# A block's scan in two or three bursts instead of four, with the small work around it chained behind the bursts

## The chip, the cores and the metric

The kernel runs on one core of a Trainium2 chip. The time is the device time of one execution in microseconds (us); three runs of the kernel before gave 1520.81, 1521.10 and 1523.07 us, median 1521.1 us. The five engines are PE (TensorE, matmuls; PEld is its loading of weights), DVE (VectorE), ACT (ScalarE), POOL (GpSimd) and SP (SyncE, which here issues DMAs). Each works through its own instructions in order and waits at semaphores for the others.

## What is computed

One layer of a hybrid model on 128 context tokens and 1024 latent tokens, 1152 in all, of width 1024, in float32. Four GLA heads (keys of 64) and four HGRN heads (keys of 128) scan the tokens forwards and backwards, and a ConvFFN follows. Per head the scan is this recurrence, with its own gates in each direction; the context tokens also give the new states:

```python
def chunk_gated_linear(q, k, v, log_f, s0):
    '''S_t = diag(exp(log_f_t)) S_{t-1} + k_t v_t^T ; o_t = S_t^T q_t'''
    ...
    scores = jnp.einsum('bhnid,bhnijd,bhnjd->bhnij', q, decay, k)
    o_intra = jnp.einsum('bhnij,bhnjv->bhniv', scores, v)
    ...
def bidir_scan(q, k_fwd, k_bwd, v, logf_fwd, logf_bwd, s0_fwd, s0_bwd):
    ...
    return o_f + flip(o_b), s_f, s_b
...
    h = rmsnorm(x, norm1) * (1 + scale1) + shift1
    mix, new_gla, new_hgrn = hybrid_mixer(h, ...)
    x = x + gate1 * mix
    h = rmsnorm(x, norm2) * (1 + scale2) + shift2
    x = x + gate2 * conv_ffn(h, ...)
```

The shifts, scales and gates come from a product of a conditioning vector with `w_ada` (1024 x 6144), in three groups A, B and C of 2048 columns. A is needed at the start, B and C after the scan.

## The kernel before

**Stages.** Up to 87 us the kernel loads the tokens, computes group A of the conditioning, normalises, and makes the first projections. From 87 to about 645 us six groups of heads are scanned (`groups`, n = 0 to 5): groups 0 and 1 are GLA with two heads each (64 rows per head), groups 2 to 5 HGRN with one head each (128 rows). Then come the output projection and the ConvFFN, which the change leaves alone.

**A block.** A group takes its 1152 tokens in three blocks of 384 (`ORDER`, from the last to the first). `levels` scans a block by a tree of seven levels, 0 to 6: at level l, runs of 2^l tokens are joined in pairs. Each level has a part on three engines. `mixed` (L917, ACT) copies the halves of the keys or queries that meet at this level into one tile `m`. `update` (L927, L929, L933, DVE) multiplies the gates of a run onto Q, the keys k and the gates fb of the next level. And PE forms the scores of the level with many matmuls of 32 output rows (L964, output `lv`); `keep` (L978, L982, DVE) puts those that belong to the level into the tile of scores S by a mask. The matmuls of two levels form a *burst* (`burst`, L948): 48 instructions in HGRN, 96 in GLA, under high priority and held behind the projection named in `anchor["paced"]`. A block has four bursts: the diagonal (called level -1) with level 0, levels 1 and 2, 3 and 4, 5 and 6.

**The fills.** Between the bursts PE works on projections: `proj_d_steps` (L625, tiles of 128x384), `proj_t_steps` (L639, v, 128x256) and later the output projection (L777, 128x512). Each tile is the sum of three products of split operands (h1h x wh, h1l x wh, h1h x wl). `stream` hands them out so that at every half slot (eight slots per block, n and bi naming the group and the block) a goal of columns is reached (`GOALS`). Their weights are loaded by SP into two `raw` buffers (`load_w`, L129, L131), rounded by ACT into `wh` (L133), and the rest computed by POOL into `wl` (L69); a `raw` buffer is free when `wl` is done.

**The small work.** After each block its state products follow (`state_steps`): for each of three chunks of 128 tokens two transposes of keys (L1025), a copy to `kt` on ACT (L1028), and the products with v (L1032), one chunk after the other, since `ps_x` has one buffer. The results update the states `st` (L1044, L1049, DVE). When a group is scanned, its outputs are formed while the next group runs (`out_steps`: L1066 to L1069, L1092, L1106, a norm on ACT and POOL, transposes L1116, products with the output gate and a store). `gates` prepares the gates and keys of the next block; in GLA it begins with two matmuls (L868) from a tile `lr` loaded by DMA. The place of this work in the slots is a table in the code, and a scheduler orders each engine from it by priority.

**The conditioning pieces.** Groups B and C come in 32 pieces of 128x1024 from `w_ada`, each loaded by `ada_load` (L1191) and multiplied by `ada_product` (L1201, four matmuls of 32 rows, eight records in the trace). They begin in group 2, one behind a burst; five go through `raw`, 27 through free buffers of the pool `v`.

Of the kernel before, what the change touches and what calls it, by code (L numbers as in the profile page):

```python
# [28 lines left out]
BURST_AHEAD = 1000  # L29
NLOW = 5  # L30
# [19 lines left out]
def kernel(ctx: ExitStack, tc: tile.TileContext, ins, outs, stop=None):  # L50
# [161 lines left out]
    seq_w_out(4, 5)  # L212
# [92 lines left out]
    pjp = pool(es1, "pj", 13)  # L305
# [299 lines left out]
    ktp = pool(es1, "kt", 2)  # L605
    mp = pool(es1, "m15", 3)
    stp = pool(es1, "stt", 23)
# [214 lines left out]
    for n in range(2, 6):  # L822
        part_g(n - 2)
        m = groups[n]
        for into, nm in ((m.f, "fj"), (m.bb, "bj"), (m.q, "qj")):
            part_cols(into, nm)
        if n % 2 == 0:
            m.vpair = groups[n + 1].vpair = []
            part_v(m.vpair)
    part_g(4)  # L830
# [27 lines left out]
    def gates(u, b):  # L858
# [3 lines left out]
        if u.gla:  # L862
            lrs = op_.tile([P, BL], F32, name="lr", tag="on")
            nc.sync.dma_start(lrs, scr_lr[b])
            pss, bcs = [], []
            for d in range(2):
                ps = ps_o.tile([P, BL], F32, name="o", tag="o")
                mm(ps, u.wup[:, d, :], lrs, start=True, stop=True)  # L868
# [29 lines left out]
        return fb, k, k0  # L898

    def levels(u, b, fb, k, k0):  # L900
# [46 lines left out]

        def burst(*parts):  # L948

            widths = [LB << max(lev - NLOW, 0) for lev, _, _ in parts]  # L950
            pss = [ps_lv.tile([P, 3 * sum(widths)], F32, name="lv", tag="lv") for _ in u.heads]
# [5 lines left out]
            with tc.high_priority(offset=BURST_AHEAD):  # L957
                for (lev, keys, src), got in zip(parts[::-1], strips[::-1]):
                    for i in range(3):
                        for j in range(P // LB):  # L960
                            js = slice(j * LB, (j + 1) * LB)
                            for ps, (r0, r1) in zip(got, u.heads):
                                with tc.issue_after(last.ins) if last is not None else nullcontext():
                                    last = mm(  # L964
                                        ps[js, i, :],
                                        keys[r0:r1, i * P + j * LB : i * P + (j + 1) * LB],
# [20 lines left out]

        k_0 = mixed(kf_, 0)
        (diag, s0), last = burst((-1, k0, q), (0, k_0, Q))
        for SL_, ps in zip(SL, diag):  # L990
            nc.scalar.activation(SL_, ps, AF.Copy, scale=2.0 if u.gla else 1.0)
        keep(0, s0)
        update(0)
        yield last
        for lev in (1, 3, 5):
            ka, qa = mixed(kf_, lev), mixed(Qf_, lev)
            update(lev)
            kb = mixed(kf_, lev + 1)
            yield last
            strips, last = burst((lev, ka, qa), (lev + 1, kb, Q))  # L1000
            for n in range(2):
                keep(lev + n, strips[n])
            update(lev + 1)
            if lev == 3:
                for S_, SL_ in zip(S, SL):
                    for j in range(LB, P, LB):
                        nc.scalar.activation(S_[j : j + LB, :, j : j + LB], SL_[j : j + LB], AF.Copy)
            if lev == 5:
# [3 lines left out]
            yield last  # L1012
        yield last

    def state_steps(u, b, k):

        tl = u.tot[b]
        for i in (2, 1, 0):
# [28 lines left out]
            if b == 0 and i == 0:  # L1047
                for c in range(7):
                    nc.vector.scalar_tensor_tensor(  # L1049
                        u.stf[c + 1],  # L1050
                        u.stf[c],
                        u.tot[c // 3][:, 1, c % 3 : c % 3 + 1],
                        u.stf[c + 1],
                        op0=ALU.mult,
                        op1=ALU.add,
                    )
# [56 lines left out]
    def out_second(u, i, b, on):  # L1113
        pt = ps_o.tile([P, BL], F32, name="o", tag="o")
        for j in range(3):
            nc.tensor.transpose(pt[:, j * P : (j + 1) * P], on[:, j, :], ident)  # L1116
# [6 lines left out]
        if u is groups[2] or u is groups[4]:  # L1123
# [11 lines left out]
    def out_steps(u):  # L1135


        if u.gla:
            for b, (first, second) in enumerate(((7, 9), (10, 12), (15, 17)) if u.tau == 0 else ((9, 11), (12, 14), (15, 17))):
                yield "half", first  # L1140
# [1291 lines left out]
```

## Time and profile before

| | |
|---|---|
| median of three runs | 1521.1 us |
| span of the profiled execution | 1515.2 us |
| of it, the scan stage | 87 to 645 us |
| PE busy in the span | 1464.7 us (97%) |
| PE busy in the scan stage | 544.62 of 558.00 us |
| bursts (L964) | 72: 12 HGRN blocks and 6 GLA blocks with four each |

A row of the profile names line, engine, operation and tiles (out<-in), and its shapes. In a timeline the first two numbers are start and duration. Matmuls are pipelined, so their durations overlap: two consecutive projections start 0.17 us apart while each lasts 0.34. How long a stretch of PE took is therefore read from one start to another. A float32 matmul leaves two records, a projection or a transpose one: a burst of 24 instructions shows as x48.

### The profile page before, as it was taken

To read this page: it belongs to the slowest core of one execution; us is meant where nothing else is said; L and a number is where in the kernel's file an instruction comes from. 1 tells how busy PE (TensorE), PEld (TensorE's weight loads), DVE (VectorE), ACT (ScalarE), POOL (GpSimd) and SP (SyncE) were. 2 spreads that over 40 slices of the span, in tenths; PEclk is the share of its full clock that TensorE was granted. 3 is DMA by queue.
4 is the path that set the end of the run, shared out by engine and by line. 5 is a ranking of instruction groups with operands and counts; after the bars stand their busy time and mean duration, and the time that the engine had idled before them with its cause. 6 is when DMAs were issued, how large, how long until landed. Compare 5 with 4: busy or idle time off the path is not lost.

```text
span 1515.2 us, 31139 instructions
## 1 busy us (share of the span) xinstructions
PE 1464.7 (97%) x12509; PEld 1247.6 (82%) x12509; DVE 1145.1 (76%) x1735; ACT 781.1 (52%) x1519; POOL 705.0 (47%) x537
## 2 busy tenths in 40 slices
PE   6999999999999999899998999999999999999998
PEld 2898998999898988777776888888888877888886
DVE  3766566565565767755699999999999999689575
ACT  3575667555455455613765444444444444466444
POOL 1602122334333241222229999999999996100001
PEclk9999999999999999999999999999999999999999
DMA  9311111335535463967642745445644567989762
GB/s 341 134 44 48 45 57 52 117 98 171 162 97 184 120 203 121 334 247 251 219 142 89 244 115 144 119 119 139 196 119 139 169 154 215 371 267 368 241 191 115
DMA packets 173802, 253.79 MB, mean 167 GB/s; under 512 B 11828, under 2 KB 113698, under 8 KB 171738
## 3 DMA queue, kind: packets, MB, share of 16 engines
q1 hardware_dynamic: 150455, 173.52, 36.0%
q0 software_dynamic: 22592, 77.60, 16.6%
q8 instruction: 98, 1.61, 0.5%
q10 hardware_dynamic: 611, 0.68, 0.1%
q14 instruction: 46, 0.38, 0.1%
HBM read 191.93 MB, written 82.90 MB: 181 GB/s over the span
## 4 chain that ended last, share of the span: by engine, by line
PE 79%; DVE 7%; DMA 5%; ACT 3%; issue 3%; POOL 2%; SPq 0%; POOLq 0%; DVEq 0%; ACTq 0%
PE u L1777 24%; PE mm L625 15%; PE xb L2279 8%; PE yb L2279 6%; PE mm L639 5%; PE x L2009 4%; PE lv L964 3%; DVE acc L1943 3%; PE mm L777 2%; PE yb L2333 2%; PE u L1544 2%; PE x L1032 1%; PE mm L519 1%; DMA raw<-in_w_in_dram 1%; PE ada L1201 1%
## 5 line engine op out<-in xcount | busy, mean ns | idle before, releaser
L1943 DVE SCALAR_TENSOR_TENSOR acc<-u,convc,acc 128x945 f32<-128x945 f32 (+2 forms) x352 | 426.9, 1218 | 8.9 <-ACT acc L1931 1.8
L69 POOL TENSOR_TENSOR wl<-raw,wh 128x1024 fp32r<-128x1024 f32 x42 | 103.0, 2466 | 249.8 <-ACT wh L133 194.2
L625 PE MATMUL mm<-h1h,wh 128*128 128x384 f32 x528 | 185.0, 350 | 1.3 <-ACT qj L528 1.3
L625 PE MATMUL mm<-h1l,wh 128*128 128x384 f32 x528 | 179.0, 339 | 0.0
L625 PE MATMUL mm<-h1h,wl 128*128 128x384 f32 x528 | 179.0, 339 | 0.0
L927 DVE TENSOR_TENSOR Q<-Q,fb 128x384 f32<-128x384 f32 x126 | 81.9, 650 | 82.4 <-PE lv L964 81.4
L69 POOL TENSOR_TENSOR wul<-sr,wuh 128x512 fp32r<-128x512 f32 (+1 forms) x64 | 115.0, 1799 | 38.6 <-ACT wuh L1759 38.6
L69 POOL TENSOR_TENSOR wul<-ra,wuh 128x1024 fp32r<-128x1024 f32 x43 | 110.0, 2559 | 6.6 <-ACT wuh L133 6.5
L917 ACT ACTIVATE m<-k 128x384 f32<-128x384 f32 x126 | 70.2, 557 | 79.9 <-DVE k L929 37.2
L2243 POOL TENSOR_TENSOR sq<-sq,mhalf 128x1 f32<-128x1 f32 x9 | 11.1, 1231 | 205.8 <-DVE sq L2242 205.8
L625 PEld LDWEIGHTS mm<-h1h,wh 128*128 128x128 f32 x528 | 99.5, 188 | 6.2 <-issue 3.9
L625 PEld LDWEIGHTS mm<-h1l,wh 128*128 128x128 f32 x528 | 99.5, 188 | 0.6 <-issue 0.2
L625 PEld LDWEIGHTS mm<-h1h,wl 128*128 128x128 f32 x528 | 99.3, 188 | 0.8 <-issue 0.5
L639 PE MATMUL mm<-wh,h1h 128*128 128x256 f32 x288 | 83.8, 291 | 1.5 <-ACT v L664 1.5
L929 DVE TENSOR_TENSOR k<-k,fb 128x384 f32<-128x384 f32 x126 | 74.2, 589 | 12.3 <-ACT m L917 7.2
L639 PE MATMUL mm<-wh,h1l 128*128 128x256 f32 x288 | 80.4, 279 | 0.0
L639 PE MATMUL mm<-wl,h1h 128*128 128x256 f32 x288 | 80.4, 279 | 0.0
L133 ACT ACTIVATE wh<-raw 128x1024 fp32r<-128x1024 f32 x50 | 52.8, 1058 | 38.5 <-PE mm L625 11.6
L1971 ACT ACTIVATE u2p<-u 128x512 f32<-128x512 f32 x44 | 26.5, 602 | 77.3 <-PE u L1777 76.7
L1759 ACT ACTIVATE wuh<-ra 128x1024 fp32r<-128x1024 f32 x42 | 44.3, 1054 | 36.6 <-issue 22.1
L2045 POOL TENSOR_TENSOR acc<-acc,acc 128x1152 f32<-128x1152 f32 x22 | 60.0, 2730 | 5.0 <-DVE acc L1943 5.0
L1759 ACT ACTIVATE wuh<-sr 128x512 fp32r<-128x512 f32 (+1 forms) x63 | 48.7, 773 | 23.1 <-PE x L2009 16.4
(385 smaller groups left out, 4464.1 us busy)
## 6 DMA issues: line engine op xcount, KB each, us to landing
ra<-in_w_ffn_up_dram SPq DMA_DIRECT2D x84, 256.0 KB, 3.5
raw<-in_w_in_dram SPq DMA_DIRECT2D x32, 512.0 KB, 4.5
v<-in_w_ada_dram SPq DMA_DIRECT2D x27, 512.0 KB, 5.1
scr_g<-acc POOLq DMA_DIRECT2D x22, 576.0 KB, 5.6
scr_s<-late POOLq DMA_DIRECT2D x11, 1024.0 KB, 4.3
scr_t<-in_w_ffn_down_dram POOLq DMA_DIRECT2D x16, 704.0 KB, 7.3
wa<-in_w_ada_dram SPq DMA_DIRECT2D x16, 512.0 KB, 5.3
scr_t<-in_w_ffn_down_dram POOLq DMA_DIRECT2D x2, 2816.0 KB, 12.5
```

The costliest lines, as they stand in the source:

```text
L69: return eng.tensor_tensor(out, full, hi.bitcast(F32), op=ALU.subtract)
L625: anchor["fill"] = mm(ps, a[:, kt, :], h[kt][b], start=(n == 0), stop=(n == 23))
L639: anchor["fill"] = mm(ps, h[kt][t // 3][:, ts_], a[:, kt % 4, :], start=(n == 0), stop=(n == 23))
L917: nc.scalar.activation(aps(t, 0, [[2 * h, NB], [h, 2], [1, h]]), aps(src, 0, [[2 * h, NB], [BL + h, 2], [1, h]]), AF.Copy)
L927: nc.vector.tensor_tensor(qm, qm, aps(ff_, 2 * h - 1, [[BL - h, 2], [2 * h, NB], [0, h]]), op=ALU.mult)
L929: nc.vector.tensor_tensor(km, km, aps(ff_, BL + 2 * h - 1, [[-(BL + h), 2], [2 * h, NB], [0, h]]), op=ALU.mult)
L1759: return lambda: nc.scalar.activation(hi, raw, AF.Copy), lambda eng: split_lo(eng, lo, raw, hi)
L1777: last = mm(dst, w_slot(c, a, x)[:, kt, :], HB[y][b][:, kt, :], start=(start and n == 0), stop=(stop and n == 11), skip_group_check=True,)
L1943: last = nc.vector.scalar_tensor_tensor(o, u3[:, r0 + dy : r1 + dy, c0 + dx : c1 + dx], wc(3 * (dy + 1) + dx + 1), o, op0=ALU.mult, op1=AL ...
L2009: last = mm(pk, HB[h]["p"][:, 4 * half + kt, :], aps(flat(W[x]), a * 512 + kt * P, [[(b - a) * 512, 2], [1, P]]), start=(half + kt + n == ...
L2045: last = nc.gpsimd.tensor_tensor(accg, accg, accu, op=ALU.mult)
L2279: anchor["down"] = mm(banks[i][:, cs], w[a][:, ts_], w[b][:, 512 + cs.start : 512 + cs.stop], start=(start and j == 0 and n == 0), stop=(j ...
```

## The change

A block's levels go in fewer bursts: a table `BURSTS` names the levels after which a burst is issued. In GLA it has levels -1 to 2, then 3 and 4, then 5 and 6; in HGRN -1 to 2, then 3 to 6. The matmuls are the same. Level 6 reads the keys themselves in place of a mixed copy. More mixed copies wait for one burst, so the pool `m15` grows from 3 to 6 buffers and `kt` from 2 to 3; `pj` (projection results) shrinks from 13 to 11 and `stt` from 23 to 18.

`state_beats` takes the place of `state_steps` up to the second block of group 4: all of a block's key transposes stand directly behind one burst and all its products behind the next, using columns of the burst's own bank beside `ps_x`. `out_beats` places the outputs of groups 0 to 3 behind bursts by a table `OUT_SLOTS`. GLA's gate matmuls stand behind a burst too, with the load of `lr` split off ahead (`gate_rank`). A conditioning piece stands behind every burst from the first block on, where one is loaded; all 32 go through `raw`, and a load is issued two slots before a burst. The weights of group 4 are loaded in another order (f first, then a gate, then bb, v, q). The low part of group 2's outputs moves from `v` to the pool `on`. The last group keeps the old placement.

```diff
+BURSTS = {True: (2, 4, 6), False: (2, 6)}
...
+    seq_cols(2080 + 2 * P)
     seq_cols(3616)
-    for c in (2080, 2592, 1568):
-        seq_cols(c + 2 * P)
+    seq_cols(2592 + 2 * P)
     seq_wide(3104 + 2 * P)
+    seq_cols(1568 + 2 * P)
...
-    pjp = pool(es1, "pj", 13)
+    pjp = pool(es1, "pj", 11)
...
-    ktp = pool(es1, "kt", 2)
-    mp = pool(es1, "m15", 3)
-    stp = pool(es1, "stt", 23)
+    ktp = pool(es1, "kt", 3)
+    mp = pool(es1, "m15", 6)
+    stp = pool(es1, "stt", 18)
...
-        k_0 = mixed(kf_, 0)
-        (diag, s0), last = burst((-1, k0, q), (0, k_0, Q))
...
-        for lev in (1, 3, 5):
-            ka, qa = mixed(kf_, lev), mixed(Qf_, lev)
-            update(lev)
-            kb = mixed(kf_, lev + 1)
-            yield last
-            strips, last = burst((lev, ka, qa), (lev + 1, kb, Q))
...
+        parts = [(-1, k0, q)]
+        for lev in range(7):
+            if lev in BURSTS[u.gla]:
+                parts.append((lev, kf_ if lev >= NLOW else mixed(kf_, lev), Q))
+                strips, last = burst(*parts)
+                yield last
...
+                parts = []
+                update(lev)
+            else:
+                parts.append((lev, mixed(kf_, lev), mixed(Qf_, lev)))
+                update(lev)
...
+    def state_beats(u, b, k, cur, slots):
...
+        yield "beat", slots[0]
+        at, x = columns()
+        for (i, c, need), to in zip(chunks, at):
+            for d in need:
+                anchor["mm"] = nc.tensor.transpose(to[d], k[:, d, i * P : (i + 1) * P], ident)
...
+        yield "beat", slots[1]
+        at, x = columns()
+        for (i, c, need), to, t in zip(chunks, at, kts):
+            for d in need:
+                for v, (r0, r1) in zip(u.v, u.heads):
+                    anchor["mm"] = mm(to[d][r0:r1], t[:, d, r0:r1], v[:, c, :], start=True, stop=True, skip_group_check=True)
...
-    def ada_load(spare=False):
+    def ada_load():
...
-            if spare:
-                piece = flat(vp.tile([P, NTILE, P], F32, name="v", tag="v"))[:, 0:1024]
...
+            piece = rawp.tile([P, 4, 256], F32, name="raw", tag="raw")
...
-                if (2, 0, 6) <= (n, bi, slot) < (5, 0, 0) and slot % 2 == 0:
-                    with tc.issue_after(last.ins):
-                        with tc.high_priority(offset=BURST_AHEAD):
-                            ada_product()
-                        ada_load(spare=(n, bi) >= (2, 2))
...
+                elif got is not None or (n == 2 and bi > 0 and slot == 4):
...
+                    with tc.high_priority(offset=BURST_AHEAD):
+                        for act in (
+                            lambda: states.step("beat", slot),
+                            ada_product,
+                            lambda: outs_.step("beat", at),
+                        ):
+                            with behind(anchor["mm"]):
+                                act()
...
+                    if n < 5 and slot + 2 in BURSTS[u.gla] and part == 1:
                         anchor["paced"] = anchor["fill"]
+                        ada_load()
```

In the order of an engine a row gives line, operation, tiles (out<-in), shape and count. First PE in group 1 (GLA), at a block's second burst. Before, levels 1 and 2 with the products of one chunk behind them; the key transposes and the gate matmul stand by themselves earlier in the projections:

```order
L1025 MATMUL x<-ident,k 128x128 x2
L868 MATMUL o<-lr,wup_2350 128x384
...
L639 MATMUL mm<-wh,h1l_402 128x256
L964 MATMUL lv<-Q,m_2211 32x32 x24
L964 MATMUL lv<-m_2206,m_2204 32x32 x24
L1032 MATMUL x<-v,kt 64x128 x4
L639 MATMUL mm<-wh,h1h_381 128x256
```

After the change, levels 3 and 4 with the products of all three chunks, a conditioning piece and the gate matmuls:

```order
L641 MATMUL mm<-wh,h1l_402 128x256
L998 MATMUL lv<-Q,m_2270 32x32 x24
L998 MATMUL lv<-m_2230,m_2228 32x32 x24
L1132 MATMUL x<-v,kt 64x128 x8
L1132 MATMUL lv<-v,kt 64x128 x4
L1297 MATMUL ada<-raw,cT 32x256 x4
L882 MATMUL o<-lr,wup_2235 128x384 x2
L641 MATMUL mm<-wh,h1h_381 128x256
```

One interruption of the projections holds what stood in several, and a conditioning piece is there in a group that had none. Next PE in group 4 (HGRN). Before, a burst of two levels with a piece and two transposes behind it:

```order
L625 MATMUL mm<-h1l_410,wh 128x384
L964 MATMUL lv<-Q,m_8145 32x32 x12
L964 MATMUL lv<-m_8140,m_8138 32x32 x12
L1201 MATMUL ada<-v,cT 32x256 x4
L1025 MATMUL x<-ident,k 128x128 x2
L625 MATMUL mm<-h1h_386,wl 128x384
```

After the change, the burst of levels 3 to 6, the products of the block before, and an output (transposes of one block, scores and states of the next):

```order
L627 MATMUL mm<-h1h_365,wl 128x384
L998 MATMUL lv<-Q,k 32x64 x12
L998 MATMUL lv<-m_7784,m_7782 32x32 x12
L998 MATMUL lv<-m_7759,m_7757 32x32 x12
L998 MATMUL lv<-m_7726,m_7724 32x32 x12
L1132 MATMUL x<-v,kt 128x128 x3
L1132 MATMUL lv<-v,kt 128x128 x2
L1226 MATMUL o<-ident,on 128x128 x3
L1176 MATMUL o<-v,S 128x128
L1178 MATMUL o<-st,Q 128x128
L1179 MATMUL o<-st,Q 128x128
```

Two bursts have become one, and full-width work follows it directly. Last, SP's DMAs in the middle of the scan. Before, pieces go to `v` and only weights to `raw`:

```order
L1191 DMA v<-in_w_ada_dram 128x4x256 x2
L131 DMA raw<-in_w_in_dram 128x8x128
L1191 DMA v<-in_w_ada_dram 128x4x256 x2
L131 DMA raw<-in_w_in_dram 128x8x128 x2
L1191 DMA v<-in_w_ada_dram 128x4x256
```

After the change both go to the two `raw` buffers in turn:

```order
L1287 DMA raw<-in_w_ada_dram 128x4x256 x2
L132 DMA raw<-in_w_out_dram 128x1024
L132 DMA raw<-in_w_in_dram 128x8x128 x3
L1287 DMA raw<-in_w_ada_dram 128x4x256
L132 DMA raw<-in_w_in_dram 128x8x128 x2
```

The second piece of SP's rows shows loads of weights and of pieces that take turns at the same two buffers.

More of the change, by code (lines that the diff above doesn't have):

```diff
@@ L1230, in stream, with behind @@
             streamed += got
+    def behind(last):
+        return tc.issue_after(last.ins) if last is not None else nullcontext()
+    OUT_SLOTS = (
+        (6, 10, 14, 18, 20, 22),
+        (10, 12, 14, 18, 20, 22),
+        (10, 14, 18, 22),
+        (10, 14, 18, 22),
+    )
     none = Steps(iter(()))
-    states, outs_, ready = none, none, None
+    states, outs_, ready, last = none, none, None, None
     for n, u in enumerate(groups):
@@ L1262 @@
                 for part in range(2):
[L1263 to L1266 removed]
+                    if n == 5:
+                        with behind(last):
+                            if part == 0:
+                                states.step("keys")
                                 while slots["held"]:
                                     slots["held"].pop(0)()
[L1269 to L1270 removed]
```

217 lines of the change are left out of this document (148 added, 69 removed).

## The prediction

> **What bounds the kernel now.** I read first where the span goes by engine, then the stage that the change touches, and then what PE waited for in it.
>
> ```profile
> PE 1464.7 (97%) x12509; PEld 1247.6 (82%) x12509; DVE 1145.1 (76%) x1735; ACT 781.1 (52%) x1519; POOL 705.0 (47%) x537
> PE 79%; DVE 7%; DMA 5%; ACT 3%; issue 3%; POOL 2%; SPq 0%; POOLq 0%; DVEq 0%; ACTq 0%
> ```
>
> PE is busy 97% of the span and carries 79% of the chain of waits. The scan, where all of the edits are, runs from 87 to 645 us; the windows view gives it in one row (span of the stretch, then PE, PEld, DVE, ACT and POOL busy with their instructions, the granted clock, the DMA share, GB/s):
>
> ```profile
> 87.00:645.00 558.00, 544.62 (x8059) 498.78 (x8058) 361.06 (x819) 317.73 (x856) 157.70 (x141) 1.00 0.39 123
> ```
>
> PE is busy 544.6 of 558 us at a granted clock of 1.00, so only 13.4 us are idle; DVE (361.1) and ACT (317.7) have a third of the stage to spare. The largest of PE's waits in the stage are small:
>
> ```profile
> PE x L1032 <- ACT kt L1028: 2.8, 5, 1.1
> PE lv L964 <- ACT m L917: 2.6, 3, 1.4
> PE ada L1201 <- DMA v<-in_w_ada_dram: 1.5, 1, 1.5
> PE mm L625 <- ACT qj L528: 1.3, 1, 1.3
> PE x L1025 <- DVE st L1044: 1.2, 2, 0.7
> ```
>
> So the scan takes what PE's instruction stream takes, and a change of order pays only if the same matmuls go through PE in less time. Busy time does not say that; start-to-start times do. In the timeline (start, duration, instruction) of a bare HGRN burst between projections:
>
> ```profile
> 431.51 0.33 PE L625 MATMUL mm<-h1l,wh 128*128 128x384 f32 x1
> ...
> 432.20 0.34 PE L625 MATMUL mm<-h1h,wl 128*128 128x384 f32 x1
> 432.46 0.46 PE L964 MATMUL lv<-Q,m 128*32 128x32 f32 x24
> 432.73 0.40 PE L964 MATMUL lv<-qj,k 128*32 128x32 f32 x24
> ...
> 433.34 0.34 PE L625 MATMUL mm<-h1l,wh 128*128 128x384 f32 x1
> ```
>
> Four projections take 432.20 − 431.51 = 0.69 us, 173 ns each. From the last one before the burst to the second behind it are 1.14 us; less two paces, the burst adds **0.80 us**. A GLA burst of 96 records stands among 128x256 projections, of which seven fill the time between the first two rows (0.83 us, 119 ns each):
>
> ```profile
> 93.66 0.28 PE L639 MATMUL mm<-wl,h1h 128*128 128x256 f32 x1
> ...
> 94.49 0.28 PE L639 MATMUL mm<-wh,h1l 128*128 128x256 f32 x1
> 94.70 0.59 PE L964 MATMUL lv<-Q,m 64*32 64x32 f32 x46
> ...
> 95.14 0.60 PE L964 MATMUL lv<-m,m 64*32 64x32 f32 x45
> ...
> 95.90 0.28 PE L639 MATMUL mm<-wl,h1h 128*128 128x256 f32 x1
> ```
>
> Inside it, 50 records start between 94.70 and 95.14: 8.8 ns each. It adds 1.41 − 0.24 = 1.17 us, of which 96 × 8.8 ns = 0.845 are records, so **0.33 us** is going into the narrow form (32 columns) and out again. For the HGRN burst the same sum gives 0.80 − 48 × 0.0088 = **0.38 us**. The records are the same before and after; this toll per visit is what the change can remove.
>
> **What goes on PE.** A conditioning piece alone (8 records, also 32 columns wide), and two transposes alone:
>
> ```profile
> 454.59 0.33 PE L625 MATMUL mm<-h1h,wl 128*128 128x384 f32 x1
> 454.86 0.64 PE L1201 MATMUL ada<-v,cT 128*32 128x256 f32 x8
> ...
> 455.71 0.33 PE L625 MATMUL mm<-h1l,wh 128*128 128x384 f32 x1
> ```
>
> ```profile
> 402.47 0.34 PE L625 MATMUL mm<-h1h,wl 128*128 128x384 f32 x1
> 402.65 0.39 PE L1025 MATMUL x<-ident,k 128*128 128x128 f32 x2
> ...
> 403.05 0.33 PE L625 MATMUL mm<-h1l,wh 128*128 128x384 f32 x1
> ```
>
> The piece adds 1.12 − 0.35 = 0.77 us; the transposes 0.58 − 0.35 = 0.23, which is two records of about 0.11: work in the full form pays no toll, so chaining transposes, 128-row products and outputs behind a burst saves nothing by itself. A chain that the kernel already has:
>
> ```profile
> 422.02 0.34 PE L625 MATMUL mm<-h1h,wl 128*128 128x384 f32 x1
> 422.28 0.54 PE L964 MATMUL lv<-Q,m 128*32 128x64 f32 x24
> 422.64 0.37 PE L964 MATMUL lv<-m,m 128*32 128x32 f32 x24
> 422.83 0.66 PE L1201 MATMUL ada<-v,cT 128*32 128x256 f32 x8
> 423.42 0.49 PE L1032 MATMUL x<-v,kt 128*128 128x128 f32 x2
> ...
> 423.93 0.34 PE L625 MATMUL mm<-h1l,wh 128*128 128x384 f32 x1
> ```
>
> It adds 1.91 − 0.35 = 1.56 us. Alone its parts are 0.80 + 0.77 + 0.23, and some 0.1 for 24 records of 64 columns, 1.90: a piece directly behind a burst shares one visit, worth 1.90 − 1.56 = 0.34 us. But 29 pieces do that already, so it is no new gain.
>
> The gain is the number of visits, counted in the two orders of PE from the first burst to the last (64-column products of GLA are a narrow form too). Before there are 82: the 72 bursts with what follows them, one of them cut in two by projections, 6 product groups alone and 3 pieces alone. After, 42 bursts remain (12 HGRN blocks × 2 and 6 GLA blocks × 3, for 18 × 4), but 20 pieces stand behind full-form transposes or products of their chain and go in a second time: 62. So 30 bursts fewer leave **20 visits fewer**, × 0.33 to 0.38 = 6.6 to 7.6 us. The GLA chains also change between narrow forms (burst, 64-column product, piece), in 12 places that this trace has nowhere. Between nothing and a whole toll each (0.33) that costs 0 to 4 us; I take 0, since the nearest row, burst to piece at 422.83, shows none, and keep 4 for the range. Interruptions of the projections by full forms fall from some 150 to 58 in all; at 0.58 − 0.35 − 2 × 0.11 = 0.01 each they give 0.6 us at most. Sum on PE: **−8 us**.
>
> [...]
>
> **What goes on the other engines.** The chains between bursts lengthen: two or three levels of mixing and updating must be ready for one burst.
>
> ```profile
> L927 DVE TENSOR_TENSOR Q<-Q,fb 128x384 f32<-128x384 f32 x126 | 81.9, 650 | 82.4 <-PE lv L964 81.4
> L917 ACT ACTIVATE m<-k 128x384 f32<-128x384 f32 x126 | 70.2, 557 | 79.9 <-DVE k L929 37.2
> ```
>
> A level costs 0.56 on ACT and 0.65 on DVE for Q; three of them and a last update are about 4.3 us, up to 8 where the key updates and other work of DVE lie between. HGRN bursts stand 10 to 14 us of projections apart afterwards (some 60 to 80 of them at 173 ns), so this is covered. In GLA's first block only 20 projections of 119 ns, 2.4 us, stand between the first two bursts: a stall of 1 to 2 us there. ACT gets one more mixed copy per HGRN block, 12 × 0.56 = 7 us in an engine idle for 240. The two waits on keys and states, 2.8 and 1.2 us, go, because products now come a whole burst behind their transposes; what is late next there is the burst itself, on m, 2.6 us, which fewer bursts make rarer. I take −4, and for the first GLA block +1.5.
>
> **The conditioning pieces** all go through the two `raw` buffers that load the weights.
>
> ```profile
> SPq L131 <- POOL wl L69: 181.3, 24, 30.1
> raw<-in_w_in_dram SPq DMA_DIRECT2D x32, 512.0 KB, 4.5
> v<-in_w_ada_dram SPq DMA_DIRECT2D x27, 512.0 KB, 5.1
> L133 ACT ACTIVATE wh<-raw 128x1024 fp32r<-128x1024 f32 x35 | 37.1, 1059 | 21.2 <-PE mm L625 11.6 <-DMA scr_wo<-wh 5.4 <-PE mm L639 1.8
> L69 POOL TENSOR_TENSOR wl<-raw,wh 128x1024 fp32r<-128x1024 f32 x35 | 85.5, 2446 | 223.5 <-ACT wh L133 167.9 <-PE mm L639 32.5 <-PE ada L1201 8.7
> ```
>
> SP waits for a `raw` buffer for 181 us already; that is prefetching and costs PE nothing. A weight holds its buffer 4.5 + 1.06 + 2.45 = 8.0 us. A piece needs 5.1 us to land, about 5.5 with its issue; its PE instruction stands in order behind a burst, so if it lands late, PE and all projections behind it wait. By the order, with projections at the paces above, a buffer comes free 3.3 and 4.0 us ahead of the use at two places in group 1; elsewhere there is time. That is 2.2 + 1.5 = +3.7 us. The 1.5 us that one piece in `v` cost goes. The new order of group 4's weights and 11 `pj` buffers in place of 13 I cost at nothing: projections of other columns cover them, and a loss would be one evacuation wait, 1.3 us by the row of the wait on qj, or a few of them.
>
> Sum: −8 − 4 + 1.5 + 3.7 − 1.5 = −8.3 us. The profiled span of 1515.2 and the median of 1521.1 differ by 5.9 us around the program, which the change leaves alone, so 1521.1 − 8.3 gives **1513 us**.
>
> **The rivals.** *The gain is given back*: fewer and longer chains also mean that one late input stops more. Five late pieces at 1.5 to 2 us would eat the 8; the time is 1518 to 1523, no change. For it: the 3.7 us above are already two such. Against: DVE and ACT have a third of the stage free.
>
> *Slower, by the two buffers*: a piece waiting for its burst holds a buffer that the next weight needs. SP issues in order, so weights behind it slip by up to 8.0 us each, the time of a whole load and split. One such slip takes the gain; from the second on the kernel is slower: −8.3 + 2 × 8.0 = +8, 1529. For it: 67 uses in place of 40 of two buffers. Against: 35 × 8 + 32 × 8 = 536 us of buffer time out of 2 × 558, if a piece waits some 3 us behind its landing.
>
> *More*: every small wait of the stage goes but 3 us, and no piece is late: −8 − 10, 1503.
>
> [...] *No effect on visits* (20 re-entries as dear as the 30 bursts saved, because of projections slipped between): the count in the order speaks against it; it would be 1521 with the waits.
>
> **How the numbers follow.** Forecast 1513 (1509 to 1517): 0.50, 0.12 of it with a toll between narrow forms. More: 0.16. Given back or no effect: 0.21. Slower: 0.13. The bound of 0.2%, about what a measurement of this kernel can tell from no change, is 3 us, 1518 to 1524: faster 0.66, same 0.21, slower 0.13. The range leaves out the slower case and the far end of more: 1504 to 1522.
>
> **What would show it.** In the changed trace: 42 bursts; the stage some 8 us shorter with busy PE shorter by about as much, since records overlap little at a toll; idle time of PE near 10 us, with waits on kt gone. Wrong would be: waits of ada or of the projections on `raw` over 8 us (the second rival), projections that wait for wl on POOL, or an equal time from first burst to last with 62 visits, which would mean that the toll is not per visit but per record or per narrow-to-narrow change.

## The result, and the profile after

The changed kernel took 1544.33 us (median of four runs, 1540.97 to 1546.28) against 1521.15 us of the kernel before on the same chip: **1.5% slower** (ratio 1.0150, 95% interval 1.0133 to 1.0167). The prediction was 1513, with 1504 to 1522 as its range.

The page and the chain of waits of the changed kernel:

```profile
PE 1470.0 (95%) x12509; PEld 1255.2 (81%) x12509; DVE 1153.4 (75%) x1735; ACT 784.5 (51%) x1541; POOL 707.7 (46%) x537
PE 72%; DVE 8%; DMA 7%; ACT 5%; POOL 4%; issue 3%; SPq 0%; POOLq 0%; ACTq 0%; DVEq 0%
```

PE's share of the chain fell from 79% to 72%; DVE, DMA, ACT and POOL have grown in it. The same stretch of the scan as before, in the windows view (PE busy first, the granted clock third from the end):

```profile
87.00:645.00 558.00, 531.33 (x7713) 492.96 (x7713) 352.52 (x775) 309.49 (x847) 158.01 (x137) 0.98 0.34 105
```

In the same 558 us PE now stands for 26.7 us instead of 13.4, carries out 7713 records instead of 8059, and its granted clock is 0.98 instead of 1.00. PE's largest waits from 80 to 680 us:

```profile
PE mm L627 <- DVE g L679: 9.7, 3, 5.1
PE ada L1297 <- DMA raw<-in_w_ada_dram: 3.8, 1, 3.8
PE mm L627 <- ACT fj L530: 3.0, 2, 1.6
PE mm L627 <- ACT qj L530: 2.9, 2, 1.9
PE x L1082 <- ACT kt L1078: 2.2, 4, 0.9
PE ada L1297 <- issue: 2.1, 2, 1.0
PE lv L998 <- issue: 1.8, 1, 1.8
```

The waits on kt that are left all stand from 648 us on, in the last group, which keeps the old placement (L1082 is a line of `state_steps`); the longest is

```profile
661.37 0.71 PE L1082 MATMUL x<-v,kt 128*128 128x128 f32 x4 [0.90 <-ACT kt L1078]
```

In the blocks with the new placement PE waits for no kt over 0.15 us. Much larger than before are the waits of projections (`mm`) for the evacuation of an earlier result, its copy out of PE's bank by ACT or DVE: 9.7 + 3.0 + 2.9 us, where the largest such rows of the kernel before are 1.5 us (v) and 1.3 us (qj). The program gives PE two banks for projections, so the third cannot start until the first is evacuated. A piece came 3.8 us late, and new are 3.9 us in which PE waited for nothing that the profile shows (`issue`).

From the start of every PE record and the list of the clock's windows the time up to the last projection of the layer can be split: pauses of PE over 150 ns, the time lost outside them in windows at half clock (estimated as half of the window, since projections started 0.32 us apart in such a window at 541 us and 0.17 at full clock), and the rest, which is PE's working time. All of it is read from one profiled execution of each kernel; that of the kernel before, with a span of 1515.2 us, was one of its faster ones.

| us from 85 on | before | after | difference |
|---|---|---|---|
| start of the last projection | 706.2 | 730.0 | +23.8 |
| pauses of PE | 15.3 | 34.2 | +18.9 |
| lost at half clock | 0.0 | 10.1 | +10.1 |
| working time | 605.9 | 600.7 | -5.2 |

The working time did get shorter, by 5.2 us where the prediction had 8. The pauses, which the prediction left about as they were, cost 18.9 us, and the clock, which it read as 1.00 and gave no term, 10.1.

One pause in full shows how the parts come together. DVE, then POOL, then PE and its clock, around 541 us:

```profile
532.87 2.26 DVE L952 TENSOR_TENSOR k<-k,fb 128x384 f32<-128x384 f32 x1
537.43 2.55 DVE L952 TENSOR_TENSOR k<-k,fb 128x384 f32<-128x384 f32 x1
540.37 0.60 DVE L679 SCALAR_TENSOR_TENSOR g<-mm,vcol,g 128x384 f32<-128x384 f32 x1
...
532.30 2.40 POOL L70 TENSOR_TENSOR wl<-raw,wh 128x1024 fp32r<-128x1024 f32 x1 [5.43 <-ACT wh L134]
537.23 2.34 POOL L70 TENSOR_TENSOR wl<-raw,wh 128x1024 fp32r<-128x1024 f32 x1
...
541.03 0.69 PE L627 MATMUL mm<-h1h,wh 128*128 128x384 f32 x1 [5.13 <-DVE g L679]
541.52 0.52 PE L627 MATMUL mm<-h1l,wh 128*128 128x384 f32 x1
541.84 0.52 PE L627 MATMUL mm<-h1h,wl 128*128 128x384 f32 x1
```

```profile
536.00:540.00 4.00, 0.00 (x0) 0.00 (x0) 3.86 (x4) 1.42 (x3) 3.54 (x2) 0.87 0.37 124
540.00:544.00 4.00, 2.97 (x38) 2.53 (x42) 2.17 (x5) 0.49 (x1) 0.00 (x0) 0.50 0.02 6
544.00:548.00 4.00, 4.00 (x101) 3.40 (x91) 3.78 (x11) 3.32 (x7) 0.00 (x0) 0.78 0.02 4
```

Two weights were split close together, the two k updates on DVE that overlapped a split lasted until 0.4 us after its end (2.26 and 2.55 us, where 0.55 is usual), the gate's evacuation stood behind them, and PE stood for 5.13 us. Then its projections started 0.32 us apart (541.84 less 541.52) instead of 0.17, until the clock came back.

### The profile page after: what moved, and what is told of

Read it like the earlier page. It is cut to its first block, busy times and chain, and to the rows that moved or that the text cites. A ratio compares the mean times of both kernels' runs of the same rounds, so it can differ in the third digit from the quotient of the medians.

```text
span 1540.8 us, 31081 instructions
## 1 busy us (share of the span) xinstructions
PE 1470.0 (95%) x12509; PEld 1255.2 (81%) x12509; DVE 1153.4 (75%) x1735; ACT 784.5 (51%) x1541; POOL 707.7 (46%) x537
## 4 chain that ended last, share of the span: by engine, by line
PE 72%; DVE 8%; DMA 7%; ACT 5%; POOL 4%; issue 3%; SPq 0%; POOLq 0%; ACTq 0%; DVEq 0%
PE u L1906 22%; PE mm L627 12%; PE xb L2408 8%; PE yb L2408 6%; PE mm L641 5%; PE x L2138 3%; PE mm L779 3%; PE lv L998 2%; DMA raw<-in_w_in_dram 2%; DVE acc L2072 2%; PE yb L2462 2%; PE u L1673 2%; POOL wl L70 1%; PE mm L521 1%; DVE k L952 1%
## 5 line engine op out<-in xcount | busy, mean ns | idle before, releaser
L952 DVE TENSOR_TENSOR k<-k,fb 128x384 f32<-128x384 f32 x126 | 86.1, 685 | 8.3 <-ACT m L940 4.9
L940 ACT ACTIVATE m<-k 128x384 f32<-128x384 f32 x108 | 60.8, 563 | 55.4 <-DVE k L952 41.1
L940 ACT ACTIVATE m<-Q 128x384 f32<-128x384 f32 x84 | 48.2, 574 | 47.1 <-DVE Q L950 40.4
L2100 ACT ACTIVATE u2p<-u 128x512 f32<-128x512 f32 x44 | 26.3, 599 | 79.1 <-PE u L1906 76.2
## 6 DMA issues: line engine op xcount, KB each, us to landing
scr_t<-in_w_ffn_down_dram POOLq DMA_DIRECT2D x2, 2816.0 KB, 13.1
```

Of the source, the lines that this page charges most:

```text
L940: nc.scalar.activation(aps(t, 0, [[2 * h, NB], [h, 2], [1, h]]), aps(src, 0, [[2 * h, NB], [BL + h, 2], [1, h]]), AF.Copy)
L952: nc.vector.tensor_tensor(km, km, aps(ff_, BL + 2 * h - 1, [[-(BL + h), 2], [2 * h, NB], [0, h]]), op=ALU.mult)
```

## The experiments

The kernel before ran beside each group; its medians were 1520.1 to 1520.8 us. The medians, with the ratio to it, and the same split as above, again of one profiled execution each:

| run | median us | ratio, 95% interval | pauses | half clock | working |
|---|---|---|---|---|---|
| e1, no piece loads | 1530.4 | 1.0048 to 1.0093 | 26.3 | 6.8 | 599.4 |
| e2, old steps | 1546.4 | 1.0159 to 1.0189 | 31.8 | 10.2 | 605.6 |
| e3, four bursts | 1530.7 | 1.0044 to 1.0082 | 22.2 | 8.2 | 607.7 |
| e4, late bias | 1545.6 | 1.0141 to 1.0186 | 36.2 | 9.2 | 602.1 |
| e5, four in GLA | 1532.7 | 1.0065 to 1.0095 | 22.7 | 10.2 | 601.3 |
| e6, four, no loads | 1521.1 | 0.9986 to 1.0013 | 13.1 | 4.9 | 605.9 |
| e7, before, raw | 1519.7 | 0.9984 to 1.0003 | 12.0 | 1.7 | 607.3 |
| e8, before, pj 11 | 1520.3 | 0.9985 to 1.0012 | 14.8 | 1.5 | 605.7 |
| e9, four in GLA, no loads | 1518.8 | 0.9974 to 0.9998 | 15.1 | 4.7 | 601.6 |
| e10, old weight order | 1542.0 | 1.0125 to 1.0161 | 33.0 | 11.3 | 600.7 |
| e11, own buffer | 1521.6 | 0.9995 to 1.0021 | 14.5 | 6.7 | 607.0 |
| e12, four, old steps | 1534.9 | 1.0076 to 1.0119 | 19.4 | 7.2 | 611.4 |
| e13, e5 with buffers apart | 1528.2 | 1.0044 to 1.0093 | 19.8 | 5.0 | 602.4 |
| e14, after, buffers apart | 1541.8 | 1.0128 to 1.0162 | 33.8 | 4.5 | 602.8 |

The single runs of a kernel with such pauses spread by up to 10 us, so differences of 2 to 3 us between them are not read.

**First group: one part each.** e1 takes the loads of the pieces away:

```diff
-            piece = rawp.tile([P, 4, 256], F32, name="raw", tag="raw")
...
-            nc.sync.dma_start(piece, src[:, half])
+            piece = [h1h[j][0].bitcast(F32)[:, 0:256] for j in range(4)]
```

> The changed kernel, except that the 32 conditioning pieces are not loaded: their matmuls read tiles of h1h that are in SBUF anyway, so the conditioning of groups B and C is not computed. Every matmul stays where it is, and the two raw buffers serve weights alone. Theory RAW (pieces and weights in two buffers arrive late, and ACT and the projections wait behind them): PE's direct waits on pieces (3.8 us and the clock that they lower) go, and so do most of the waits on projection results that stand on ACT behind a late weight; 12 to 20 us less than the changed kernel, 1525 to 1532. Theory LUMPS (work chained behind bursts reaches ACT and DVE in lumps, and the results of projections wait behind them, since PE has two banks for them): only the direct waits go, 4 to 7 us, 1537 to 1540.

1530.4 us, 14 us less, inside what RAW gave. The late piece and the pause of 5.1 us at 541 us are gone with the loads; the waits for fj (2.8 us) and a wait for g at 219 us (2.7 us) stayed, and two new ones of 2.7 and 2.9 us came. What ACT waited for in front of `wh`, the rounding of a weight, in the kernels before, after and e1 (total, times, longest):

```profile
ACT wh L133 <- DMA raw<-in_w_in_dram: 1.0, 1, 1.0
```

```profile
ACT wh L134 <- DMA raw<-in_w_in_dram: 16.7, 10, 2.7
```

```profile
ACT wh L134 <- DMA raw<-in_w_in_dram: 1.2, 1, 1.2
```

Before, weights lay in `raw` when ACT came to them; after, ACT stood ten times until the load landed, and everything behind it on ACT stood too. In the changed kernel, for example:

```profile
523.36 1.06 ACT L134 ACTIVATE wh<-raw 128x1024 fp32r<-128x1024 f32 x1 [2.71 <-DMA raw<-in_w_in_dram]
524.33 0.47 ACT L530 ACTIVATE qj<-mm 128x384 f32<-128x384 f32 x1
...
524.85 0.44 PE L627 MATMUL mm<-h1h,wh 128*128 128x384 f32 x1 [1.09 <-ACT qj L530]
```

The evacuation of qj stood behind the late weight, and PE behind the evacuation.

e2 spreads the small work as before, with the changed bursts, pools and pieces (core of the edit; the outputs of groups 2 and 3 come seven slots later, and GLA's gates at slot 5, without priority):

```diff
+                with behind(last):
+                    outs_.step("half", at)
+                    states.step("product")
                 if n == 5:
-                    with behind(last):
-                        outs_.step("half", at)
-                        states.step("product")
+                    pass
...
-            if (n, bi) < (4, 2):
+            if False:
...
-        if n < 4:
+        if False:
```

> The changed kernel with its bursts, pools, raw buffers and pieces behind bursts, but the state products, outputs and gates are spread between projections as before (state_steps and out_steps in all groups; the outputs of groups 2 and 3 seven slots later, because their gate weights come later now). LUMPS: the waits on projection results (some 15 us with the clock) go and the saved visits partly stay; 1524 to 1532. RAW: no gain, 1540 to 1548, since pieces and weights are as they are.

1546.4 us: no gain. That the chained work alone makes the pauses is refuted; they are 31.8 us without it too. They are partly others, though. The waits for evacuations fell, as LUMPS said (g from 9.7 to 4.7 us, qj from 2.9 to 1.1, fj from 3.0 to none), but PE waited more for kt (4.1 us), for weights (3.2) and for nothing (5.8), and the working time rose by 4.9 us.

e3 gives every block its four bursts back, with a second table for the chained work (not shown: `anchor["paced"]`, the projection behind which a burst is held, is set ahead of each of the four):

```diff
-BURSTS = {True: (2, 4, 6), False: (2, 6)}
+BURSTS = {True: (0, 2, 4, 6), False: (0, 2, 4, 6)}
+BEATS = {True: (2, 4, 6), False: (2, 6)}
...
-                elif got is not None or (n == 2 and bi > 0 and slot == 4):
+                elif (got is not None and slot in BEATS[u.gla]) or (n == 2 and bi > 0 and slot == 4):
```

> The changed kernel with four bursts per block as before, everything else at its place (chained work and pieces behind the same bursts, levels 2, 4, 6 in GLA and 2, 6 in HGRN). If the toll per visit is what the prediction says, 30 more visits cost 30 x 0.33 to 0.38 = 10 to 11 us in the projections' pace and nothing else changes: 1552 to 1556. Theory CHAIN (longer chains between fewer bursts make the waits): the waits on projection results go with the shorter chains, and the time falls below 1540.

1530.7 us, 14 us faster than with two or three. The working time rose by 7.0 us for 31 more visits (93 against 62, counted as in the prediction), 0.23 each. But pauses and clock fell by 14: the fewer bursts did harm. (In the profiled execution of e3, 1533.5 us, the last projection starts 6.9 us earlier than the changed kernel's, which is 13.9 less 7.0.)

e4 moves the end of conditioning group C to group 5, since ACT stood at its bias DMAs during the pause at 541 us:

```diff
+            finish.append(g)
+            if g == "B":
+                ada_finish()
...
+                if (n, bi, slot) == (5, 0, 2):
+                    ada_finish()
```

> The changed kernel, except that the last step of conditioning group C (clear a tile, two bias DMAs issued on ACT, one sum) is issued in group 5 instead of behind the last piece. In the changed kernel ACT stood 5.3 us at these DMAs, waiting for the clearing on DVE, which POOL's wl splits held, and PE waited 5.1 us and then ran at half clock for two windows. All theories: that wait and its cold windows go, 7 to 9 us, 1535 to 1538. If it returns elsewhere with the same size, the cause is not this step but the state of the queues there.

1545.6 us; the pause stayed, with 5.37 us at 543 us behind the same evacuation. The step that ACT stood at was not its cause.

**Second group: where each of the two sits.** e5 has four bursts in GLA and two in HGRN (the edit of e3 with `BURSTS = {True: (0, 2, 4, 6), False: (2, 6)}`); e6 is e3 with the edit of e1; e7 is the kernel before with all pieces in `raw`:

```diff
-                if (2, 0, 6) <= (n, bi, slot) < (5, 0, 0) and slot % 2 == 0:
+                if n < 5 and slot in ((2, 4, 6) if u.gla else (2, 6)):
...
-                        ada_load(spare=(n, bi) >= (2, 2))
...
+                        if slot + 2 in ((2, 4, 6) if u.gla else (2, 6)):
+                            ada_load()
```

> The changed kernel with four bursts per block in GLA and two in HGRN, chained work and pieces behind the same bursts. In the changed kernel PE stood still three times (1.8, 1.0 and 1.0 us, nothing waited for) in or behind GLA's first burst of four levels, never behind one of two, and the first time was followed by a window at half clock. Theory LONG RUNS (a run of 192 small records and more outruns the supply of instructions): these 3.9 us and the window of about 1.7 us go, six visits more cost 6 x 0.23 = 1.4 us by the run with four bursts everywhere; 1538 to 1541. Theory CHAIN in HGRN (its longer chains make the rest of the waits): nothing else gets better here. If GLA is the whole of what four bursts gained, 1531 to 1534.

> The changed kernel with four bursts everywhere and no loads of pieces (their matmuls read h1h; conditioning B and C is not computed). Alone, each of the two edits gave 14 us. If they remove different waits, their sum: 1515 to 1519, under the kernel before, since the chaining saves visits. If both only loosen the same coincidences of late evacuations, 1524 to 1530.

> The kernel before with one part of the change alone: all 32 pieces go through the two raw buffers, from the first block on, behind the bursts of the changed kernel's table and loaded two slots ahead; v is not used for them. Theory RAW in its simple form (two buffers for 64 loads make weights and pieces late): 1529 to 1535, with waits on pieces and on weights behind ACT. If RAW needs the chains of the change, 1519 to 1524.

> The kernel before_raw of the same group with 11 instead of 13 buffers for projection results. If a result that finds no buffer is what the waits on evacuation (qj, fj, g, v) come from, 4 to 10 us above e7; if not, within 2 us of e7.

e5: 1532.7 us, 11.6 us less than the changed kernel, so nearly all that four bursts gain is gained in GLA. That is more than LONG RUNS gave by itself (1538 to 1541). The waits on nothing (`issue`) are gone; they are 3.9 of the 11.5 us by which the pauses fell. A second part went with them: in the changed kernel projections of group 1 wait 5.1 us for evacuations (g at 219 us, fj at 247 and 261 us), in e5 0.7 us. These waits stand, with 4.9 to 6.2 us, in every kernel that has GLA's three bursts together with the chained work (after, e1, e4, e10, e14), with and without the loads. With four bursts, or with the work spread (e2), they are at most 1.4 us. So it is the two together that make them; by what way was not tried.

e6: 1521.1 us, 23 us less, of the 28 that the two edits gave alone: just above the range for different waits, and under that for shared ones. Its pauses are down to 13.1 us, less than those of the kernel before. e7: 1519.7 us: RAW in its simple form falls. The same loads through the same buffers cost the kernel before nothing, although ACT waits for late weights there too (15.5 us in the row below). PE's waits for evacuations on ACT stayed at 0.9 and 0.8 us there (both v); why so little of the lateness reaches PE is open.

```profile
ACT wh L133 <- DMA raw<-in_w_in_dram: 15.5, 8, 3.7
```

e8's text speaks of e7 with 11 `pj` buffers; the kernel that ran is the kernel before with that one edit (`pool(es1, "pj", 11)`). At 1520.3 us it shows that the smaller pool costs nothing there; with the pieces in `raw` it was not tried by itself.

**Third group: sums and one candidate each.** e9 is e5 with the edit of e1. e10 puts the weights and projections of group 4 back in their old order. e11 gives the pieces one buffer of their own, in the kernel with four bursts:

```diff
-    mp = pool(es1, "m15", 6)
+    mp = pool(es1, "m15", 3)
+    pcp = pool(es1, "pc", 1)
...
-            piece = rawp.tile([P, 4, 256], F32, name="raw", tag="raw")
+            piece = pcp.tile([P, 4, 256], F32, name="pc", tag="pc")
```

e12 has the edits of e2 and e3 together.

> The run e5 (four bursts in GLA, two in HGRN, chained) with the pieces not loaded, so without conditioning B and C. LONG RUNS took 11.6 us and the loads 14.0; if these are the two causes, what is left is the saved visits (69 for 82) against a few waits: 1517 to 1521. If HGRN's two bursts make waits of their own beside the loads, 1524 or more.

> The changed kernel with one part undone: the weights and projections of group 4 in the order of before (gate of group 2 first, then f, bb, q, v). In the changed kernel the waits at 337 to 344 and 524 to 541 us (9.7 us, and four half-clock windows) stand where these weights are split and the gate is projected. Theory ORDER (the new order puts a gate with evacuations on ACT and DVE where weights are late): 8 to 14 us less, 1530 to 1536. Theory RAW (any order, since pieces delay the loads): within 3 us of 1544.

> Four bursts everywhere with the chained work, and the pieces loaded into one buffer of their own (paid by m15 with 3 in place of 6): a complete kernel. The two raw buffers serve weights alone, so if RAW is right it runs like the same kernel without the loads (1521): 1519 to 1524, with at most some waits on pieces in GLA, where 5 us stand between bursts. If not the buffers but the DMA traffic of the pieces made the waits, 1528 to 1533 as with raw.

> Four bursts everywhere, state products, outputs and gates spread as before (the edits of e2 and e3 together), pieces through raw. It has the bursts and the small work of the kernel before, and of the change only the pieces in raw, the pools and the order of group 4's weights. The kernel before with the pieces in raw ran at 1519.7. If the chained work is what lets late weights hurt, 1519 to 1524. If the order of group 4's weights or the pools do, 1528 to 1535.

e9: 1518.8 us. The changed kernel's 1544.3 less 11.6 (GLA's bursts) less 14.0 (loads) is 1518.7: the two account for the loss. What is left of the change is a gain of some 2 us (0.3 to 4.0 by the interval), hardly to be told from none, in a kernel that leaves out the loads of the pieces, which the kernel before has. e10: 1542.0 us, the order of the weights is not it. e11: 1521.6 us against e3's 1530.7, the time without the loads, with all loads done, and with `m15` back at 3 buffers: not the bytes but the buffers cost the time. Nor is the order of SP's queue enough. In e11 SP stood 144.0 us at pieces whose buffer was not free, with the weights behind them, and ACT waited only once for a weight (7.0 us):

```profile
SPq L1289 <- PE ada L1299: 144.0, 26, 16.5
```

e12: 1534.9 us, which refutes that the chained work is what lets late weights hurt: with spread work and four bursts ACT waits 33.9 us for weights.

**Fourth group: how the buffers do it.** e13 (on e5) and e14 (on the changed kernel) keep the two buffers apart during the scan, one for weights and one for pieces:

```diff
-    rawp = pool(es_w, "raw", 2)
+    raws = [pool(es_w, "raw", 1), pool(es_w, "rawb", 1)]
...
+            k = (1 if name in ("piece", "modr") else 0) if self.apart else self.n % 2
+            return raws[k].tile(shape, dt, name=name, tag=tag)
```

> The run e5 (four bursts in GLA, two in HGRN, chained) with the two raw buffers kept apart during the scan: one takes only weights, the other only pieces; the memory, the number of loads and their order in the program are the same. Theory HELD (two pieces in a row hold both buffers until their bursts come, and no weight can be loaded meanwhile): the loads' 14 us go, 1517 to 1523, the time of the same kernel without the loads (1518.8). Theory QUEUE (SP issues in order, so a piece that waits for its buffer stops the weight behind it all the same) or TRAFFIC (the bytes themselves): 1528 to 1534, as e5.

> The changed kernel itself with the two raw buffers kept apart in the same way, nothing else. HELD: the waits on late weights go, 1528 to 1533, as without the loads (1530.4); the stand-still in GLA's bursts of four levels stays. QUEUE or TRAFFIC: 1541 to 1546.

e13 gained 4.5 us of 14, with single runs from 1524.6 to 1534.3 us; e14's 2.5 us are within what is not read. Both lie where QUEUE or TRAFFIC put them, but e11 speaks against these two. Pieces that hold both buffers are at most a part of it. The row of late weights is as long as in e5 (21.0 us):

```profile
ACT wh L146 <- DMA raw<-in_w_in_dram: 21.1, 10, 3.2
```

With one buffer for weights, a load begins only when the split before it is done, so the edit takes from the weights what it gives them, and does not test HELD alone. Together with e11, where weights have both buffers and pieces a third (7.0 us late, 1521.6), this says that in these kernels weights need two buffers of their own to arrive ahead.

## Why the prediction was wrong

- **What bounds the kernel**: right that PE's stream sets the scan. But the 13.4 us of idle were carried over to the changed kernel, which has 26.7 us in the same stretch.
- **The toll per visit**: the mechanism held, the size did not. The term of 20 visits was sized at 0.33 to 0.38 us, from bare bursts between projections; runs that differ only in bursts give 0.23 (31 visits, e3 against after), 0.27 (24, e3 against e5) and 0.18 (24, e6 against e9). The working time fell by 5.2 us for the 8 of the sum. The toll of zero for full forms (0.01 each) was too small: with the same 93 visits, e12 with 150 interruptions of the projections works 3.7 us longer than e3 with 82, 0.05 each. Twenty visits at 0.18 to 0.27 us and 94 fewer interruptions (58 for 152) at 0.05 would be 8 to 10 us, not 5.2. What took the other 3 to 5 us was not settled; a toll between narrow forms (0 to 4 us in the range, with a chance of 0.12) was not tried by itself, and no run shows it. (Such changes are 18 in the trace of before and 23 in that of the changed kernel, from the first burst to the last.)
- **Waits on keys and states, −4**: the mechanism held, the size did not. Where the change moves the products, the waits went; but of the 2.8 + 1.2 us only 1.1 (kt at 228 us) and 0.7 (a state at 385 us) stood there in the kernel before. The rest stood in the last stretch, whose placement the change keeps, and there the waits stayed (kt 2.2 us).
- **The pieces' late arrivals, +3.7**: right in size and group, one of 3.8 us in group 1's last block (284 us), where two of 2.2 and 1.5 us were foreseen. That the sum comes out so near is luck.
- **The step that failed**: "SP waits for a `raw` buffer for 181 us already; that is prefetching and costs PE nothing". The sentence is true of the kernel before; the wrong step was to keep it for the kernel after. That wait was the lead of the loads; with 27 more loads in the same buffers ACT found a weight not landed ten times in place of once (16.7 us for 1.0). The rival *Slower, by the two buffers* named this place, with its price of a whole load (8.0 us) and 1529, at 13%. The price arrived in another form: ten late weights of up to 2.7 us, in front of evacuations on ACT, and the late piece; with the half clock behind the pauses 14 us in all (e1). So the sign named for it, waits of ada or of the projections on `raw` over 8 us, did not show (3.8 us). And the step fails only together with other parts of the change: in the kernel before, the same 27 loads in the same buffers cost nothing (e7).
- **What no step had**: GLA's bursts of four levels, 11.6 us (e5). Records were priced at 8.8 ns whatever the length of the run; in three of GLA's six runs of 192, PE stood 1.0 to 1.8 us besides. The chained work behind these bursts made projections wait for evacuations, 5.1 us. And half clock after a pause, 10.1 us in all: it turned the pause of 1.8 us into a loss of 3.5 and that of 5.1 us into some 7.5, by the windows' overlap.
- **Longer chains**: the 1.5 us for GLA's first block are near the 1.77 us that PE stood at 95 us, by luck: that pause lies inside the block's first burst, not ahead of the second, and PE waited for nothing in the trace, not for Q or m. Ahead of the second burst, at 100 us, it did not wait.
- **11 pj buffers and the order of group 4 at nothing**: nothing speaks against it, as far as it was tried (e8 in the kernel before, e10 in the changed one).
- The 5.9 us around the span were wrong as well: the changed kernel's profiled execution took 1542.7 us for a span of 1540.8, so 1.9 us lie around it; the rest lay between the profiled execution of before and the median of its runs. It moves nothing here.

Two things stay open: why late weights on ACT hurt the kernel before so little (e7) and the same kernel with the changed pools, pacing and weight order so much (e12), and by what way GLA's three bursts and the chained work together make projections wait for evacuations. No complete kernel of these is faster than the kernel before by more than the spread (e7 and e11 equal it); e9, which does not load the pieces, puts the worth of the fewer HGRN bursts and the chains at some 2 us, hardly more than nothing.

## What to carry to other kernels

A queue that waits for a buffer is not a spare queue: the wait (here 181 us of SP) is the lead with which its loads arrive, and whoever puts more loads through the same buffers must ask what stands behind a late one, on every engine that takes part (here ACT's rounding, late ten times for 16.7 us, then the evacuations, then PE's two banks). Whether it hurts depends on the rest of the kernel, as e7 shows, so it is to be tried. An engine that is 97% busy has no room for pauses of 2 us: price each with the half-clock window that may follow (here 3.41 us behind a pause of 1.77). And a price per small instruction, read from short runs, is to be measured again at the length of run that a change makes (here 8.8 ns at 96 records, and at 192 pauses of 1.0 to 1.8 us besides in three of six runs).

## What the runs showed of the hardware

**PE stood in and behind long runs of small instructions.** The first burst of four levels, in the timeline, and the instruction queue of the DMA view in the window from 92.7 to 93.9 us (packets, MB, share of the engines). The burst has 192 records, two for each of 96 matmuls; by that count a burst of two levels, called 48 and 96 instructions above, is 24 matmuls in HGRN and 48 in GLA:

```profile
92.36 1.00 PE L998 MATMUL lv<-m,m 64*32 64x32 f32 x90
...
93.19 0.24 PE L998 MATMUL lv<-qj,kj 64*32 64x32 f32 x5
95.21 0.70 PE L998 MATMUL lv<-qj,kj 64*32 64x32 f32 x41 [1.77 <-issue]
```

```profile
q8 instruction: 1, 0.02, 5.3%
```

A block of 16384 bytes moved on that queue from 92.78 us on for 1.02 us, the only transfer of that window, and PE stood 1.77 us, until 1.41 us after the block's end. At 152 and 187 us the same happened behind such a burst: 1.04 and 1.01 us, with a block from 1.6 and 1.3 us ahead of the pause on, until 1.50 and 1.34 us after its end. The waits of PE for nothing in e2 and e10, which have runs of 192 records too, are three each: 4.3 us for two at bursts and 1.5 us at a product in e2, 2.2 us at a burst and 1.9 us for two at pieces in e10. With bursts of 96 in GLA the kernel before and e7 have one of 0.3 us each from 85 to 640 us, and e5 shows none. What PE waited for is not shown: the trace does not name the engine that a block is for. That the pauses hang on these blocks is the author's estimate from the times above. That a long run outruns the supply of instructions, as LONG RUNS has it, no run shows; e5 shows that without the long runs the pauses are not there.

**Half clock with pauses of 1 to 5 us.** Around the same place the granted clock, third from the end:

```profile
92.00:96.00 4.00, 2.23 (x196) 2.05 (x200) 2.72 (x6) 1.12 (x3) 0.00 (x0) 0.90 0.02 4
96.00:100.00 4.00, 4.00 (x27) 3.10 (x23) 1.09 (x6) 1.18 (x5) 0.00 (x0) 0.67 0.45 134
100.00:104.00 4.00, 4.00 (x118) 2.98 (x118) 2.44 (x9) 1.95 (x6) 0.00 (x0) 1.00 0.25 51
```

The trace's list of clock windows has them at 0.50 and 3.41 us, or two together at 6.83. In the changed kernel one began at 95.20 us, as PE started again behind the pause of 1.77 us, and one at 344.38 us, 0.55 us after the end of a pause of 2.44 us; pauses of 1.86 and 2.15 us were followed by none. In those of 3.78 and 5.13 us two together began before PE started again (at 282.94 and 538.94 us, 1.32 and 2.09 us ahead). One, from 651.6 us on, came behind several short pauses, the longest of 0.98 us. What decides whether a pause brings one is not shown.

**DVE instructions took longer beside a split on POOL.** From 87 to 645 us 24 DVE instructions of the kernel before and 30 of the changed one lasted over 0.8 us longer than the median of their line and tiles, 40 and 50 us in all, and each of them overlaps a POOL tensor operation, `wl` (2.4 us) in 24 of 24 and 27 of 30 cases, as the two k updates at 533 and 537 us do. The kernel before has 40 us of this too, so what matters seems to be what stands behind: at 541 us two k updates, held 1.7 and 2.0 us, stood ahead of the evacuation that PE waited for.
